# One decoder layer on a NeuronCore: the last projection block of head 0 moved ahead of the product that spreads the running maximum

## The chip, the cores and the metric

The kernel runs on one core of a Trainium2 chip, in one launch. The metric is the device time in microseconds (us): the median of three runs, beside the time and the trace of one profiled execution. The engines are called PE (TensorE, matrix products), DVE (VectorE), ACT (ScalarE), POOL (GpSimd) and SP (SyncE, which issues most DMAs). Each takes its instructions in a fixed order and waits on semaphores for the others.

## The reference, cut to what matters

One layer of a decoder, 512 positions by 1024 channels. A mixer with two groups of heads is followed by a feed-forward part with a short convolution. The group that the change touches is the mLSTM group: 4 heads of 256 channels, in chunks of 128 positions, stabilised by a running maximum.

```python
q_, k_, v_, i_, lf_ = inp
b = jnp.cumsum(lf_, axis=-1)
dmat = jnp.where(causal, b[..., :, None] - b[..., None, :] + i_[..., None, :], -jnp.inf)
m_t = jnp.maximum(b + m[..., None], jnp.max(dmat, axis=-1))
...
scores = jnp.einsum("bhtd,bhsd->bhts", q_, k_) * jnp.exp(dmat - m_t[..., None])
...
h = num / jnp.maximum(jnp.abs(den), jnp.exp(-m_t))[..., None]
...
h = rms_norm(h, ml_norm_g[l].reshape(H, Dh)).reshape(Bsz, S, D_ML)
h = (h * jax.nn.sigmoid(o_pre.astype(jnp.float32))).astype(x.dtype)
```

q, k and the output gate o_pre come from one projection of the normed input; q and k pass a causal convolution of width 4. The other group is a gated causal convolution of width 31 over 1024 channels.

## The kernel before, in words

Nearly everything is kept in 32 bits; a projection multiplies split operands, three matmuls for one product (`mm3`, L186 to L190: high by high, high by low, low by high). A weight piece of 512 columns is split by ACT into its high part (L170) and by POOL into its low part (L171).

The order of PE and of SP is the order in which the program is written. On DVE, ACT and POOL the instructions are put in order at build time, by a planner that estimates when each can run and that prefers what stands earlier in the program. What lies in a stretch of lowered priority (`tc.cur_priority += LATER`) fills gaps: above all the convolution of width 31 (L641 to L677), of whose 31 taps 25 for each block of channels are DVE instructions on L661, one after the other into a PSUM bank `cv`, while 5 run on ACT (L655) and POOL (L657) and one on ACT alone (L649); the sums ydl (L671), ysum and ysq follow. The resulting order is fixed in the program: at run time an engine never skips a waiting instruction.

Around the change, in the order of PE:

- `head_proj(0, 0)` to `head_proj(0, 2)`: a block of 24 matmuls each, for q and k of head 0. A block's result lies in one of four PSUM banks (`mm`); q and k are then convolved by ACT and DVE (`conv4`, L412 to L415), and a gate block (the fifth and sixth) only gets a tanh on ACT (L442, tile `so`).
- `fcum` (L550): the cumulated forget gates; DVE makes `ga` from them (L553). `head_proj(0, 3)`.
- `aT` (L558): `ga` is turned; DVE finds the running maximum `Mr` by a scan (L560), ACT and DVE write its high and low part into `Ms` (L562, L563). `head_proj(0, 4)`.
- `mtok` (L568): the maximum per position; from it DVE and ACT make `em` (L570 to L572).
- `make_E(0)` (L531 to L542): the product `Mb` (L533) spreads row 0 of `Ms` over 128 partitions, into one of two PSUM banks of the kind `at`; DVE adds the causal mask (`Md`, L535); ACT makes seven exponentials `E` from `Md` and `Mb` (L540, L542).
- `head_proj(0, 5)`: the last block of head 0, its second gate block.
- Then the loop over heads (L705): the blocks of head 1 alternate with the steps of `attention(0)`. The first of these are the score products `s` (L455, in `at` banks), which DVE multiplies into `E` (L456), and the products `o` (L466). ACT reads these, POOL makes the factor `fac` (L477 to L479), DVE scales the four tiles `hn` with it (L482), and PE turns them (`hT`, L488). The blocks for v of head 1 stand before and after `hT`.

Of the kernel before, what the change touches and what calls it, by code (L numbers as in the profile page):

```python
# [52 lines left out]
def decoder_layer(ctx, tc, w_glu0, x, c, adaT, vecs, w_glu, w_qko, w_v0, w_v, w_out, w_up, w_down, out):  # L53
# [30 lines left out]
    def slot(name, dt=F32):  # L84
        return slots.tile([P, T], dt, tag="t", name=name)

    def mmbank(name):
        return psum.tile([P, T], F32, tag="mm", bufs=4, name=name)

    def atbank(name):  # L90
        return psum.tile([P, T], F32, tag="at", bufs=2, name=name)
# [265 lines left out]
    def proj(ps, pieces, off):  # L357
        for k in range(KT):
            mm3(ps, blk(pieces, off + k), u[k], k == 0, k == KT - 1)
# [48 lines left out]
    def conv4(ps, i, name):  # L408

        t = slot(f"{name}c")  # L410
        w = lambda tap: vcol("qk_conv_w", tap * 16 + i)
        S.activation(t, ps, AF.Identity, bias=vcol("qk_conv_b", i), scale=w(3))  # L412
        for d in range(1, 4):
            V.scalar_tensor_tensor(out=t[:, d:], in0=ps[:, : T - d], scalar=w(3 - d), in1=t[:, d:], op0=ALU.mult, op1=ALU.add)
        S.activation(t, t, AF.Silu)  # L415
        return t
# [13 lines left out]
    def head_proj(h, i):  # L430

        pieces, qs, ks, so = heads[h]
        ps = mmbank(f"qko{h}_{i}")
        proj(ps, pieces, i * KT)
        e = 2 * h + i % 2
        if i < 2:
            qs.append(conv4(ps, e, f"q{h}_{i}"))
        elif i < 4:
            ks.append(conv4(ps, 8 + e, f"k{h}_{i}"))
        else:  # L440
            t = slot(f"so{h}_{i}")
            S.activation(t, ps, AF.Tanh, scale=0.5)  # L442
            so.append(t)
# [76 lines left out]
    def head_tiles(name, dt, three=None):  # L520
        three = three or [slots.tile([P, T], dt, tag="t", name=f"{name}{i}") for i in range(3)]
        return [three[s][:, a : a + n] for (s, a), n in zip(PLACE, NS)]
# [8 lines left out]
    def make_E(h):  # L531
        mb = atbank(f"Mb{h}")
        PE.matmul(mb, rowsel[:, h : h + 1].to_broadcast([P, P]), Ms, start=True, stop=True)  # L533
        md = slot(f"Md{h}")
        V.tensor_tensor(out=md.rearrange("p (t m) -> p t m", t=NT), in0=mb.rearrange("p (t m) -> p t m", t=NT),  # L535
                        in1=cmask[:, None, :].to_broadcast([P, NT, P]), op=ALU.add)
        E[h] = head_tiles(f"E{h}", F32)
        for cc in range(NT):
            b = ga[:, cc, h : h + 1]
            S.activation(E[h][cc][:, :P], md[:, cc * P : (cc + 1) * P], AF.Exp, bias=b, scale=-1.0)  # L540
            if cc < NT - 1:
                S.activation(E[h][cc][:, P:], mb[:, (cc + 1) * P :], AF.Exp, bias=b, scale=-1.0)  # L542
# [28 lines left out]
    S.activation(em, em, AF.Exp, scale=-1.0)  # L571
    V.tensor_scalar(out=em, in0=em, scalar1=EPS**0.5, scalar2=None, op0=ALU.mult)  # L572

    make_E(0)
    head_proj(0, 5)


    RD = float(D) ** 0.5
# [632 lines left out]
```

## Time and profile before

| | us |
|---|---|
| median of 3 runs (lowest to highest) | 786.16 (785.89 to 786.79) |
| profiled execution, its own time | 785.76 |
| its span, first to last instruction | 784.0 |
| PE busy in the span | 762.9 (97%) |
| DVE busy | 591.6 (75%) |
| ACT busy | 408.1 (52%) |
| POOL busy | 383.9 (49%) |

Times in the views are counted from the start of the span. In a timeline a row gives start, duration, engine, line, operation and tiles, with a count when like instructions follow each other, and in brackets the idle time of the engine before it and what ended that. In the view of stretches of time each engine has its busy time and the number of its instructions, and the granted clock of PE stands before the DMA's share.

### The profile page before, as it was taken

Reading aid. Unit: us, or ns where it says so; the run is one execution under the profiler, and the core shown is the slowest. Engines: PE = TensorE matmul, PEld = TensorE weight load, DVE = VectorE, ACT = ScalarE, POOL = GpSimd, SP = SyncE. Lnnn points to the kernel's source line nnn. Section 1 sums busy time; section 2 is a strip of 40 time slices with the busy share of each in tenths; the row PEclk is TensorE's granted clock in tenths of the full one; section 3 lists DMA queues with packets and bytes.
Section 4 is the critical chain, followed back from the end, with each engine's and each line's share of the span. In section 5 each row is a group of like instructions: output and inputs, shape, how many; then the busy total and the mean of one; then the engine's idle time right before and its main releaser. Section 6 shows DMA issues by size and latency. Waiting matters only on the chain.

```text
span 784.0 us, 10572 instructions
## 1 busy us (share of the span) xinstructions
PE 762.9 (97%) x3683; PEld 636.5 (81%) x3683; DVE 591.6 (75%) x938; ACT 408.1 (52%) x766; POOL 383.9 (49%) x313
## 2 busy tenths in 40 slices
PE   7899999899999999999999999999999999999995
PEld 4678888678978888888888998888888888888884
DVE  6659999999998532565868798666555687698996
ACT  6566437667765544572244445444444444456752
POOL 3689758779779544334661446444544440000001
PEclk9999999999999999999999999999999999999998
DMA  8974213302116422334953763332333321778862
GB/s 292 326 274 145 93 71 108 134 28 107 54 54 234 165 89 104 114 110 155 398 176 124 253 217 135 128 123 81 120 114 128 128 91 58 279 257 259 285 222 107
DMA packets 35977, 124.28 MB, mean 159 GB/s; under 512 B 4146, under 2 KB 5586, under 8 KB 29908
## 3 DMA queue, kind: packets, MB, share of 16 engines
q1 hardware_dynamic: 24084, 95.15, 34.7%
q10 hardware_dynamic: 11840, 28.46, 10.2%
q8 instruction: 29, 0.48, 0.2%
q14 instruction: 24, 0.20, 0.1%
HBM read 112.17 MB, written 11.42 MB: 158 GB/s over the span
## 4 chain that ended last, share of the span: by engine, by line
PE 72%; DVE 17%; DMA 4%; ACT 3%; POOL 2%; issue 1%; SPq 0%; DVEq 0%; POOLq 0%; ACTq 0%
PE up L189 10%; PE up L190 10%; PE up L188 10%; DVE cv L661 8%; PE p L190 4%; PE p L189 4%; PE p L188 4%; PE glu L189 3%; DMA wglu<-in_w_glu 2%; PE glu L190 2%; PE glu L188 2%; PE mixa L190 2%; PE mixa L188 2%; PE mixa L189 2%; PE mixb L190 2%; PE mixb L189 2%
## 5 line engine op out<-in xcount | busy, mean ns | idle before, releaser
L661 DVE SCALAR_TENSOR_TENSOR cv<-gt,cvw,cv 128x506 f32<-128x506 f32 (+24 forms) x200 | 134.1, 727 | 0.4
L617 POOL TENSOR_TENSOR ro0r<-ro0t,mhalf 128x1 f32<-128x1 f32 x1 | 0.9, 926 | 125.9 <-DVE ro0t L615 125.9
L171 POOL TENSOR_TENSOR wup_1024l<-wup,wup_1024h 128x512 fp32r<-128x512 f32 x20 | 27.3, 1367 | 31.7 <-ACT wup_1024h L170 31.7
L171 POOL TENSOR_TENSOR wup_0l<-wup,wup_0h 128x512 fp32r<-128x512 f32 x20 | 27.8, 1388 | 29.9 <-ACT wup_0h L170 29.9
L657 POOL TENSOR_TENSOR cs<-cs,cs 128x510 f32<-128x510 f32 (+3 forms) x32 | 41.9, 1308 | 0.2
L171 POOL TENSOR_TENSOR wup_1536l<-wup,wup_1536h 128x512 fp32r<-128x512 f32 x20 | 28.1, 1405 | 27.4 <-ACT wup_1536h L170 27.4
L189 PE MATMUL up<-u2l,wup_0h 128*128 128x512 f32 (+1 forms) x100 | 36.5, 365 | 0.2 <-DVE u2l L830 0.2
L188 PE MATMUL up<-u2h,wup_0h 128*128 128x512 f32 (+1 forms) x100 | 36.6, 366 | 0.0
L188 PE MATMUL up<-u2h,wup_1024h 128*128 128x512 f32 (+1 forms) x100 | 36.5, 365 | 0.0
L190 PE MATMUL up<-u2h,wup_0l 128*128 128x512 f32 (+1 forms) x100 | 36.4, 364 | 0.0
L190 PE MATMUL up<-u2h,wup_512l 128*128 128x512 f32 (+1 forms) x100 | 36.4, 364 | 0.0
L190 PE MATMUL up<-u2h,wup_1536l 128*128 128x512 f32 (+1 forms) x100 | 36.4, 364 | 0.0
L188 PE MATMUL up<-u2h,wup_1536h 128*128 128x512 f32 (+1 forms) x100 | 36.4, 364 | 0.0
L189 PE MATMUL up<-u2l,wup_1024h 128*128 128x512 f32 (+1 forms) x100 | 36.4, 364 | 0.0
L189 PE MATMUL up<-u2l,wup_1536h 128*128 128x512 f32 (+1 forms) x100 | 36.4, 364 | 0.0
L188 PE MATMUL up<-u2h,wup_512h 128*128 128x512 f32 (+1 forms) x100 | 36.4, 364 | 0.0
L189 PE MATMUL up<-u2l,wup_512h 128*128 128x512 f32 (+1 forms) x100 | 36.4, 364 | 0.0
L190 PE MATMUL up<-u2h,wup_1024l 128*128 128x512 f32 (+1 forms) x100 | 36.4, 364 | 0.0
L155 DVE SCALAR_TENSOR_TENSOR junk<-ada,cb 128x1024 bf16<-128x1024 f32 x20 | 31.3, 1565 | 6.4 <-DMA ada<-in_adaT 6.2
L171 POOL TENSOR_TENSOR wup_512l<-wup,wup_512h 128x512 fp32r<-128x512 f32 x20 | 27.2, 1361 | 14.6 <-ACT wup_512h L170 14.6
L655 ACT ACTIVATE cs<-gt,cvw 128x511 f32<-128x511 f32 (+4 forms) x40 | 27.2, 712 | 4.5 <-POOL cs L657 3.8
L171 POOL TENSOR_TENSOR wqko_1024l<-wqko,wqko_1024h 128x512 fp32r<-128x512 f32 x12 | 16.6, 1382 | 22.4 <-PE v L189 12.3
(1061 smaller groups left out, 2685.1 us busy)
## 6 DMA issues: line engine op xcount, KB each, us to landing
wup<-in_w_up SPq DMA_DIRECT2D x22, 1024.0 KB, 7.0
wqko<-in_w_qko SPq DMA_DIRECT2D x12, 1024.0 KB, 5.0
ada<-in_adaT ACTq DMA_DIRECT2D x20, 512.0 KB, 5.9
ada<-in_adaT SPq DMA_DIRECT2D x16, 512.0 KB, 5.9
wo<-in_w_out SPq DMA_DIRECT2D x8, 1024.0 KB, 9.0
spare<-in_adaT ACTq DMA_DIRECT2D x12, 512.0 KB, 7.5
wglu<-in_w_glu SPq DMA_DIRECT2D x5, 1024.0 KB, 8.4
wd<-in_w_down SPq DMA_DIRECT2D x6, 768.0 KB
```

The lines of the kernel that those rows point to most:

```text
L155: t = V.scalar_tensor_tensor(out=junk, in0=r, scalar=1.0, in1=cb, op0=ALU.mult, op1=ALU.mult, accum_out=mod[:, i : i + 1])
L171: (eng or G).tensor_tensor(out=lo[:, :n], in0=src, in1=hi[:, :n].bitcast(F32), op=ALU.subtract)
L188: PE.matmul(ps, a[0], b[0], start=start, stop=False)
L189: PE.matmul(ps, a[0], b[1], start=False, stop=False)
L190: PE.matmul(ps, a[1], b[0], start=False, stop=stop)
L617: G.tensor_tensor(out=r, in0=t, in1=mhalf[:, :1], op=ALU.pow)
L655: S.activation(t[:, d:], cvx[j][:, : T - d], AF.Copy, scale=w(CK - 1 - d))
L657: G.tensor_tensor(out=side[:, d:], in0=side[:, d:], in1=t[:, d:], op=ALU.add)
L661: last_tap = V.scalar_tensor_tensor(out=cp[:, d:], in0=cvx[j][:, : T - d], scalar=w(CK - 1 - d), in1=cp[:, d:], op0=ALU.mult, op1=ALU.add)
```

## The change

One call moves. `head_proj(0, 5)` is written ahead of `make_E(0)` instead of behind it; no instruction is added or taken away.

```diff
     S.activation(em, em, AF.Exp, scale=-1.0)
     V.tensor_scalar(out=em, in0=em, scalar1=EPS**0.5, scalar2=None, op0=ALU.mult)
 
+    head_proj(0, 5)
     make_E(0)
-    head_proj(0, 5)
```

## The prediction

> **What bounds the kernel now.** I read the page first, then who waited for whom on PE (TensorE), then the timelines of PE and DVE (VectorE) around the edited lines, and last the chain that ended last between 150 and 270 us. On the page:
>
> ```profile
> span 784.0 us, 10572 instructions
> PE 762.9 (97%) x3683; PEld 636.5 (81%) x3683; DVE 591.6 (75%) x938; ACT 408.1 (52%) x766; POOL 383.9 (49%) x313
> DVE  6659999999998532565868798666555687698996
> ```
>
> PE looks like the bound of the whole, 97%. But the DVE row, in slices of 19.6 us, stands at 9 from the fourth slice to the thirteenth: from 59 to 255 us DVE is full as well. The edit lies at 150 to 161 us, inside that stretch. Who waited for whom on PE:
>
> ```profile
> PE Mb L533 <- DVE Ms L563: 2.4, 1, 2.4
> ...
> PE hT L488 <- ACT E L542: 0.4, 1, 0.4
> PE up L189 <- DVE u2l L830: 0.2, 1, 0.2
> ```
>
> The rows left out are waits of the opening. So in the body PE has one real stop: the product of L533 that spreads the running maximum, which waits for Ms. The PE timeline shows it and what follows:
>
> ```profile
> 150.73 1.05 PE L568 MATMUL mtok<-ident,Mr 4*128 4x4 f32 x8
> 154.16 0.77 PE L533 MATMUL Mb<-Ms,rowsel 128*128 128x512 f32 x1 [2.38 <-DVE Ms L563]
> 154.73 0.63 PE L188 MATMUL qko<-uh,wqko_1024h 128*128 128x512 f32 x1
> ...
> 157.16 0.40 PE L188 MATMUL qko<-uh,wqko_1024h 128*128 128x512 f32 x1
> 157.39 0.39 PE L189 MATMUL qko<-ul,wqko_1024h 128*128 128x512 f32 x1
> ...
> 161.25 0.39 PE L188 MATMUL qko<-uh,wqko_0h 128*128 128x512 f32 x1
> ```
>
> The stop costs more than its 2.38 us. Between the start of Mb (154.16) and 157.16 stand Mb and six matmuls of the last block: 3.00 us for seven, where the usual step between two starts is 0.23 us (157.16 to 157.39), 1.6 for seven. So 1.4 us go to a slow clock, which the windows of 3.4 us show as granted (the figure of 1.00, then 0.50, before the DMA columns):
>
> ```profile
> 150.20:153.60 3.40, 1.58 (x11) 1.14 (x9) 3.37 (x5) 3.40 (x7) 2.56 (x3) 1.00 0.00 0
> 153.60:157.00 3.40, 2.83 (x7) 2.29 (x8) 3.37 (x7) 0.95 (x3) 0.23 (x1) 0.50 0.46 154
> 152.00:211.00 59.00, 56.84 (x274) 47.57 (x275) 58.94 (x94) 41.34 (x84) 46.04 (x39) 0.97 0.20 72
> ```
>
> The third row is the one that decides: from 152 to 211 us PE is busy 56.84 of 59.00, and DVE 58.94. DVE has nothing to spare there, and its order is fixed. At the end of that stretch PE needs DVE:
>
> ```profile
> 205.63 5.20 DVE L661 SCALAR_TENSOR_TENSOR cv<-gt,cvw,cv 128x501 f32<-128x501 f32 x8
> 210.75 1.12 DVE L482 TENSOR_SCALAR hn<-hn,fac 128x256 f32<-128x256 f32 x4
> 211.57 1.12 PE L488 MATMUL hT<-ident,hn 128*128 128x128 f32 x8
> ```
>
> The transposes of head 0 (hT, L488) read the four scaled tiles hn (L482), which DVE writes from 210.75 to 211.87, behind eight convolution taps (L661). PE starts them at 211.57, while DVE is still at the last tiles: at this place PE and DVE come out level. The chain that ended last says the same; between 150 and 270 us its longest pieces are DVE's taps:
>
> ```profile
> 160.60 7.66 DVE cv L661 x12
> 205.70 5.13 DVE cv L661 x8
> ```
>
> **The change, part by part.** The last block of head 0's projections (24 matmuls, head_proj(0, 5)) now stands ahead of make_E(0): Mb, the masked copy Md on DVE, seven exponentials E on ACT (ScalarE). In the order of the built program PE's only move is Mb from before these 24 to after them; SP's order does not change, so no DMA moves; on POOL (GpSimd) two neighbours change places. DVE keeps its order but for Md, which falls seven places back, behind em (L572) and six convolution taps. ACT does the last gate (so, L442) and three others ahead of the exponentials.
>
> *The stop.*
>
> ```profile
> 137.71 1.29 POOL L171 TENSOR_TENSOR wqko_1536l<-wqko,wqko_1536h 128x512 fp32r<-128x512 f32 x1
> 152.34 1.68 DVE L563 TENSOR_TENSOR Ms<-Mr,Ms 4x512 fp32r<-4x512 f32 x1
> ```
>
> When mtok ends (151.78) PE can start its 24 matmuls at once; the last piece of their weights was split by 139.00. The 18 of them that ran at full clock took 161.25 - 157.16 = 4.09, 0.227 each, so Mb is reached at 151.8 + 24 x 0.227 = 157.2. Ms is ready at 154.02 and Mb no longer waits. PE wins 2.38 + 1.4 = 3.8 us at 161.25.
>
> *The exponentials come later.*
>
> ```profile
> 157.98 0.69 DVE L535 TENSOR_TENSOR Md<-Mb,cmask 128x512 f32<-128x512 f32 x1
> 159.31 0.39 ACT L540 ACTIVATE E<-Md,ga 128x128 f32<-128x128 f32 x1
> 161.26 0.40 ACT L540 ACTIVATE E<-Md,ga 128x128 f32<-128x128 f32 x1
> 166.66 0.63 ACT L170 ACTIVATE wqko_1536h<-wqko 128x512 fp32r<-128x512 f32 x1 [2.09 <-PE qko L189]
> 168.40 0.81 PE L455 MATMUL s<-q_0c,k_2c 128*128 128x384 f32 x2
> 169.47 0.68 DVE L456 SCALAR_TENSOR_TENSOR E<-s,E 128x512 f32<-128x512 f32 x1
> ```
>
> Twelve taps take 7.66 us (the chain, above), 0.64 each. Md now comes after six of them and em: from 157.98 that is 3.8 + 0.7, so 162.5 to 163.2. The seven exponentials take 161.66 - 159.31 = 2.35 us and end near 165.5. Mb is done by 157.6, so Md holds up nothing on DVE. Behind the exponentials on ACT stand two weight pieces of head 1; the second started at 166.66 after 2.09 us of idleness, which takes the delay. Two things need the exponentials. DVE's product E (169.47) has 4 us in hand. The second score product of PE (168.40) must take over Mb's bank, since there are two banks of that kind, so it waits until ACT has read Mb for the last time, 0.3 before the end, 165.2. PE would come there at 168.40 - 3.8 = 164.6 and waits 0.6. This new wait is paid out of the 3.8: 3.2 are left.
>
> *What is late next.* With 3.2 us in hand PE runs to hT and arrives at 208.4. The hn tiles are where DVE's fixed order puts them, and DVE had no idle time to close (58.94 of 59.00, the same instructions). So PE waits there some 3 us, and of the 3.8 us nothing is left. The stop has moved from 152 to 208; in between DVE sets the pace.
>
> *The clock at the new stop.*
>
> ```profile
> 266.77 0.44 PE L488 MATMUL hT<-ident,hn 128*128 128x128 f32 x2 [0.42 <-ACT E L542]
> ```
>
> The old stop of 2.38 us halved the clock for the next 3.4 us, and that cost was covered, since PE was ahead of hn anyway. The new stop is longer, and what follows it on PE is back to back up to 266.77, where the one other wait is 0.42 us (hT <- E). Price by the rows above: 1.4 us lost after a stop, less 0.4 idle that absorbs it, so 1.0. Its ends: 0, if the clock is not halved or the work finds more cover, and half of a whole window, 1.7, less 0.4, so 1.3. I take 1.0, since the row of the old stop is the nearest and the new stop is longer. The Trainium skill ("TensorE: Matmul & The Clock Gate", HAM oscillation) asks for a PE idle gap of more than about 3.4 us before the clock falls. The trace disagrees, since 2.38 us sufficed; by the rule this stop of some 3 us would cost nothing, a rival below.
>
> *DVE's own time.* The same work can take longer or shorter by where it meets POOL:
>
> ```profile
> 158.03 1.29 POOL L657 TENSOR_TENSOR cs<-cs,cs 128x510 f32<-128x510 f32 x1
> 159.28 1.29 POOL L675 TENSOR_TENSOR ysq<-ysq,ydl 128x512 f32<-128x512 f32 x1
> 159.87 0.73 DVE L572 TENSOR_SCALAR em<-em 128x16 f32<-128x16 f32 x1
> L671 DVE SCALAR_TENSOR_TENSOR ydl<-ysum,gt x3: 683/1091/1456, 156.0 to 196.5; 128x512 f32<-128x512 f32 x3
> 196.16 1.28 POOL L171 TENSOR_TENSOR wqko_1536l<-wqko,wqko_1536h 128x512 fp32r<-128x512 f32 x1 [0.17 <-ACT wqko_1536h L170]
> 196.53 1.46 DVE L671 SCALAR_TENSOR_TENSOR ydl<-ysum,gt 128x512 f32<-128x512 f32 x1
> ```
>
> em has 16 columns and takes 0.73 us: it ends at 160.60, with the POOL instruction that runs since 159.28. The three ydl (L671) have one shape and take 0.68, 1.09 and 1.46; the last, at 196.53, ends with its compute 0.55 us after the POOL instruction that began at 196.16. So a DVE instruction whose operands all lie in SBUF waits for the POOL instruction that runs. The Trainium skill ("SBUF — State Buffer", Who interferes with whom) says so too: one port pair is locked for a whole instruction, and whoever issues first holds it; the rows agree, and by it the sum moves with the phase. Without Md ahead of it em comes 0.6 us earlier, at 159.27, within 0.02 us of the moment when POOL changes instructions (159.28): it saves 0.57 or ends where it did, with Md's 0.6 still to come. But ydl at 196.53 has 0.9 us of waiting in it, and a shift of DVE by half a microsecond either way vanishes there. I take 0; the ends are -1.2 (em, and the 0.41 that ydl of 1.09 holds, and then some, saved) and +1.0 (one more POOL turn of 1.25 lost, less some).
>
> **The sum.** Profiled execution 785.76 us (span 784.0 and 1.8 around it): PE -3.8, the bank +0.6, the wait for hn +3.2, the clock +1.0, DVE 0: +1.0, so 786.8. The median of the runs shown, 786.16, is 0.4 above the profiled one; on that footing 787.1.
>
> **The rivals.**
> 1. The stop moves, but its slow clock costs nothing (the window falls well, or the rule cited holds): 786.2. For it: the clock row is a single case. Against it: a shorter stop was enough.
> 2. DVE meets POOL better at em and at ydl, hn lands 1.2 us earlier, PE's stop shrinks to under 2 us and the clock costs some 0.3: 785.3.
> 3. Slower: DVE loses a POOL turn on its way to hn, most likely at the ydl near 180 us (1.09) by asking just after POOL has started; it decides if hn's first tile starts after 211.2. hn +1.0, PE's stop 4 us, its clock +1.0: 788.2.
> 4. The gain survives, since something lets hn come earlier by as much: 786.16 - 3.2 = 783.0. It would need idle time on DVE between 152 and 211 us, of which the window shows 0.06 us. A change that doesn't do what it says is excluded by the order: Mb does stand behind the 24 matmuls.
>
> **How the numbers follow.** My forecast (stop moved, clock paid) 50%, rival 1 13%, rival 2 12%, rival 3 19%, rival 4 6%. About 0.2%, 1.6 us, is what a measurement of this kernel can tell from no change: below 784.6 or above 787.7. Faster: rival 4 and a little of rival 2, 7%. Slower: most of rival 3 and the upper tenth of my own case, whose clock cost reaches 1.3 and DVE up to half a microsecond more, 28%. Within: 65%. The range from 785.3 (rival 2) to 788.5 (rival 3 with a full window) leaves out rival 4 and the tails. The likeliest time is 787.1.
>
> **What would show it.** Right: no wait at L533 for Ms; matmuls at 0.23 from 152 on; a wait of about 0.6 at L455 for E L542; a wait of 2.5 to 4 us at L488 for hn (L482) near 211 us; a granted clock of 0.5 in the 3.4 us around or after it; hn within 0.5 us of 210.75; no wait or a smaller one at 266. Wrong: PE without a stop at L488, or hn moved by more than 1.5 us, or the end moved by over 2 us with the stop as described.

## The result, and the profile after

| | before | after |
|---|---|---|
| median, first comparison | 786.10 us (7 runs) | 783.52 us (7 runs, 782.93 to 784.42) |
| ratio of the runs, 95% interval | | 0.9973 (0.9964 to 0.9983) |
| median, second comparison, on another occasion | 785.49 us (35 runs) | 783.53 us (11 runs) |
| ratio, 95% interval | | 0.9985 (0.9973 to 0.9996) |
| profiled execution, its span | 785.76, 784.0 us | 782.93, 781.2 us |

The kernel became faster: its median is lower by 2.6 us in the first comparison and by 2.0 in the second. The ratios, which weigh all runs, give less, 2.1 and 1.2 us, with 95% intervals of 1.3 to 2.8 and 0.3 to 2.1. The forecast was 787.1, no change to speak of. The page of the changed kernel, with the rows that were shown of before:

```profile
span 781.2 us, 10573 instructions
PE 762.0 (98%) x3683; PEld 635.5 (81%) x3683; DVE 590.7 (76%) x938; ACT 407.6 (52%) x766; POOL 384.8 (49%) x313
DVE  6659999999999433555868798666555678698986
```

On these rows almost nothing differs. Who waited for whom on PE from 100 us on:

```profile
PE hT L488 <- DVE hn L482: 1.4, 1, 1.4
PE hT L488 <- ACT E L542: 0.2, 1, 0.2
PE up L189 <- DVE u2l L830: 0.2, 1, 0.2
```

The stop at Mb is gone, a stop at hT has come, as forecast, but of 1.4 us and not of some 3. The PE timeline, and the granted clock in the windows (before the DMA's columns):

```profile
149.76 1.05 PE L568 MATMUL mtok<-ident,Mr 4*128 4x4 f32 x8
150.74 0.50 PE L188 MATMUL qko<-uh,wqko_1024h 128*128 128x512 f32 x1
...
156.34 0.40 PE L533 MATMUL Mb<-Ms,rowsel 128*128 128x512 f32 x1
...
208.62 1.46 PE L488 MATMUL hT<-ident,hn 128*128 128x128 f32 x8 [1.35 <-DVE hn L482]
```

```profile
150.20:153.60 3.40, 3.40 (x18) 2.88 (x18) 3.37 (x4) 2.56 (x5) 2.32 (x2) 1.00 0.04 10
153.60:157.00 3.40, 3.40 (x16) 2.82 (x15) 3.37 (x8) 1.75 (x3) 1.19 (x1) 1.00 0.38 145
152.00:211.00 59.00, 57.65 (x292) 48.07 (x291) 58.97 (x99) 40.31 (x85) 45.31 (x38) 1.00 0.20 72
```

PE runs at full clock throughout, and its busy time in the stretch is the whole of it less the stop. DVE is as full as before (58.97 of 59.00). Now the DVE timeline, the rows that decide; first those of after, then two of before that the prediction did not show:

```profile
147.53 1.20 DVE L560 TENSOR_TENSOR_SCAN Mr<-aT,zero 4x512 f32<-4x512 f32 x1
158.31 0.17 DVE L572 TENSOR_SCALAR em<-em 128x16 f32<-128x16 f32 x1
160.95 0.69 DVE L535 TENSOR_TENSOR Md<-Mb,cmask 128x512 f32<-128x512 f32 x1
179.13 0.69 DVE L671 SCALAR_TENSOR_TENSOR ydl<-ysum,gt 128x512 f32<-128x512 f32 x1
194.58 0.80 DVE L671 SCALAR_TENSOR_TENSOR ydl<-ysum,gt 128x512 f32<-128x512 f32 x1
208.13 1.13 DVE L482 TENSOR_SCALAR hn<-hn,fac 128x256 f32<-128x256 f32 x4
```

```profile
148.52 1.20 DVE L560 TENSOR_TENSOR_SCAN Mr<-aT,zero 4x512 f32<-4x512 f32 x1
180.66 1.09 DVE L671 SCALAR_TENSOR_TENSOR ydl<-ysum,gt 128x512 f32<-128x512 f32 x1
```

The same instructions, but three of them are shorter: em 0.17 instead of 0.73, the ydl 0.69 instead of 1.09 and 0.80 instead of 1.46. That is 0.56 + 0.40 + 0.66 = 1.62 us. From the scan Mr to hn it is 208.13 - 147.53 = 60.60 us, and was 210.75 - 148.52 = 62.23: 1.63 us, the same. In the kernel before hT began 0.82 us behind hn's start, now 0.49: 0.33 more. So hT starts 1.96 us earlier from Mr. But hT itself now takes longer: it reads the hn tiles as they come, and the matmul behind it follows after 1.22 us instead of 0.88; first before, then after:

```profile
212.45 0.36 PE L188 MATMUL v<-wv_0h,uh 128*128 128x256 f32 x1
```

```profile
209.84 0.36 PE L188 MATMUL v<-wv_0h,uh 128*128 128x256 f32 x1
```

That matmul comes 63.93 us after Mr before and 62.31 after, 1.62 us earlier, just as hn. This is what the change brings in these profiles, and both intervals hold it. The two profiled executions differ by more, 2.83 us. Of that 0.99 lies ahead of Mr, in the opening, which the change doesn't touch; over the thirteen profiles of this study Mr began between 147.27 and 149.48, and in one with PE's order of before it began at 147.53 as well. Another 0.20 lies at the next hT, whose wait for E was 0.42 us and is 0.22, and which goes up and down between 0.22 and 0.46 us in all profiles but one.

### The profile page after: what moved, and what is told of

The parts are those of the page before. It is cut to its first block, busy times and chain, and to the rows that moved or that the text cites. A ratio compares the mean times of both kernels' runs of the same rounds, so it can differ in the third digit from the quotient of the medians.

```text
span 781.2 us, 10573 instructions
## 1 busy us (share of the span) xinstructions
PE 762.0 (98%) x3683; PEld 635.5 (81%) x3683; DVE 590.7 (76%) x938; ACT 407.6 (52%) x766; POOL 384.8 (49%) x313
## 4 chain that ended last, share of the span: by engine, by line
PE 80%; DVE 14%; DMA 2%; ACT 1%; POOL 1%; issue 1%; SPq 0%; DVEq 0%; POOLq 0%; ACTq 0%
PE up L189 10%; PE up L188 10%; PE up L190 10%; DVE cv L661 6%; PE p L190 4%; PE p L188 4%; PE p L189 4%; PE glu L189 3%; PE glu L190 3%; PE glu L188 3%; PE qko L188 3%; PE qko L189 3%; PE qko L190 3%; PE mixa L190 2%; PE mixa L188 2%; PE mixa L189 2%
```

## The experiments

Theory A: from Mr to hT DVE's fixed line sets the pace, and the gain is what DVE's line got shorter; PE's removed stop makes room. Theory B: the gain is PE's removed stop itself. In the kernels with a changed order, VectorE's, ScalarE's and GpSimd's lines are written down instruction by instruction, so that only the named exchange differs; inserted source lines shift the line numbers behind them by two or three. Since the opening varies, I read hn and hT from the start of Mr (where PE waits at hT, hT itself takes some 0.3 us longer, as above, so for those kernels the column of hn is the better measure):

| run | median us | ratio to before (95%) | Mr to hn | Mr to hT | stop at hT |
|---|---|---|---|---|---|
| before | 785.5 to 786.1 | | 62.23 | 63.05 | 0 |
| after | 783.52 | 0.9973 (0.9964 to 0.9983) | 60.60 | 61.09 | 1.35 |
| after again | 783.53 | 0.9985 (0.9973 to 0.9996) | 60.63 | 61.12 | 1.39 |
| em late | 783.90 | 0.9988 (0.9974 to 1.0001) | 61.16 | 61.65 | 1.36 |
| one more tap | 784.45 | 0.9990 (0.9980 to 0.9999) | 61.82 | 62.31 | 1.39 |
| DVE half alone | 786.27 | 1.0005 (0.9992 to 1.0019) | 62.54 | 63.36 | 0 |
| PE +1.3 late | 783.68 | 0.9972 (0.9960 to 0.9984) | 60.60 | 61.09 | 0 |
| PE +1.36 early | 784.07 | 0.9993 (0.9970 to 1.0016) | 60.61 | 61.09 | 0.20 |
| PE +3.86 early | 785.37 | 0.9995 (0.9981 to 1.0009) | 62.41 | 63.22 | 0 |
| after, Ms early | 782.88 | 0.9968 (0.9954 to 0.9983) | 59.61 | 60.09 | 0.52 |
| after, three exchanges | 781.58 | 0.9949 (0.9937 to 0.9961) | 57.80 | 59.38 | 0 |
| before, Ms early | 783.20 | 0.9971 (0.9955 to 0.9987) | 60.20 | 60.69 | 1.19 |
| before, three exchanges | 781.83 | 0.9970 (0.9942 to 0.9998) | 58.36 | 59.32 | 0 |

**The changed kernel again.**

> The changed kernel once more, as the yardstick of the other runs on this chip. Theory A (from 152 to 211 us VectorE's in-order line sets the pace; the gain is VectorE's, 0.57 us at em L572 and 0.41 and 0.66 us at two ydl L671, and TensorE's removed stop only makes room for it) and theory B (the gain is TensorE's removed stop itself, 2.38 us plus 1.4 us of halved clock, less what it waits for hn) both expect 783.5 us, 2.6 below the kernel before. Theory C (a different opening, up to about 45 us, that varies from run to run, makes a third of the difference) expects the profile's VectorE times at Ms L563 to differ from the first profile by some tenths of a us while em keeps its 0.17 us; the ratio would then lie nearer 0.9977 (1.84 us).

em, the ydl, hn and the stop come out within 0.04 us of the first profile. The median is what A and B expected; the ratio is nearer what theory C expected, since three of the eleven runs took over 785 us. The profiled execution is one of them: 785.29 us, 2.4 more than the first, and 0.6 of that lies in the opening. Most of the rest lies at 400 us, where PE waits 1.25 us for `gains`; the DVE timeline of this run, then that of the first:

```profile
397.63 1.22 DVE L782 SCALAR_TENSOR_TENSOR gains<-mod,vec 128x8 f32<-128x8 f32 x1
398.76 1.33 DVE L784 COPY gains<-mod 128x8 f32<-128x8 f32 x1
```

```profile
396.24 1.21 DVE L782 SCALAR_TENSOR_TENSOR gains<-mod,vec 128x8 f32<-128x8 f32 x1
397.38 0.16 DVE L784 COPY gains<-mod 128x8 f32<-128x8 f32 x1
```

A copy of 8 columns takes 0.16 or 1.33 us; DVE also came to this place 0.8 us later, counted from hT. Theory C is right in that other places than the change scatter from run to run, the opening being one and this another.

**em one tap later.**

```diff
 DVE: cv4 tap 128x493, cv5 tap 128x500
-em (L572)
 cv4 tap 128x492
+em (L572)
```

> The changed kernel with one step of VectorE's line exchanged: em L572 stands behind the tap that followed it, so it is asked for 0.64 us later, inside GpSimd's ysq L675. No work is added. Theory A: em takes about 0.7 us instead of 0.17, hn L482 comes at least 0.55 us later, TensorE's stop at hT L488 grows from 1.35 to about 1.9 us, and the end comes 0.5 us later (784.0); up to 1.6 us later (785.1) if the two ydl fall back as well. Theory B: 783.5, as without the exchange.

```profile
158.79 0.70 DVE L572 TENSOR_SCALAR em<-em 128x16 f32<-128x16 f32 x1
...
179.52 0.68 DVE L671 SCALAR_TENSOR_TENSOR ydl<-ysum,gt 128x512 f32<-128x512 f32 x1
```

em takes 0.70, hn comes 0.55 us later from Mr, and hT by as much (61.65 against 61.11, the mean of the two runs of after). The medians differ by 0.4 us, which alone would not be told from nothing. An exchange without added work costs what em's wait costs. The stop did not grow to 1.9: its row in the waits of PE says where the time went, to the wait for E that the prediction had priced at 0.6.

```profile
PE s L455 <- ACT E L542: 0.4, 1, 0.4
```

**One more tap on DVE.**

```diff
             last_tap = V.scalar_tensor_tensor(out=cp[:, d:], ...)
+            if (j, d) == (5, 11):
+                more = V.scalar_tensor_tensor(out=cp[:, d:], in0=cvx[j][:, : T - d], scalar=zero[:, :1], in1=cp[:, d:], op0=ALU.mult, op1=ALU.add)
```

> The changed kernel with one more tap (scalar zero, 0.64 us, operand in PSUM) in VectorE's line ahead of em L572, where Md stood before: VectorE then meets GpSimd at em and ydl as in the kernel before, with TensorE's stop at L533 still gone. This is the case of the prediction. Theory A: em 0.73 us, ydl 1.09 and 1.46 us again, hn 2.3 us later than in the changed kernel, the stop at hT grows from 1.35 to about 3.6 us, a halved clock of some 3.4 us behind it: 785.8 without that, up to 787.2 with it. Theory B: 783.5, nothing of it on TensorE's line.

hn comes 1.2 us later and so does hT, and the median is 0.9 above the changed kernel; theory B had nothing. But the 2.3 us were too much:

```profile
159.26 0.56 DVE L572 TENSOR_SCALAR em<-em 128x16 f32<-128x16 f32 x1
...
180.48 0.67 DVE L674 SCALAR_TENSOR_TENSOR ydl<-ysum,gt 128x512 f32<-128x512 f32 x1
```

em waited again, ydl did not: GpSimd's line at that place moved together with DVE's. So the ydl are not short because DVE comes earlier. Nor did the stop grow (1.39), since PE was held up at L455 by 1.1 us already.

**DVE's half of the change alone.**

```diff
 DVE, in the kernel before (PE: Mb, then head_proj(0, 5)):
-Md (L535)
 cv4, cv5 taps, em (L572), four more taps
+Md (L535)
```

ScalarE's and GpSimd's lines are the changed kernel's too, but for the place of the last gate on ScalarE. Md moves by six taps, not by the eight that the expectation names.

> The kernel before (TensorE's order untouched, Mb L533 ahead of the block) with the changed kernel's order on VectorE and GpSimd: Md L535 eight taps later and behind em L572, and on ScalarE the exponentials behind two side taps and a split. The half of the change that is VectorE's alone. Theory A: em and ydl get shorter and hn comes some 1.6 us earlier, but TensorE, 0.33 us behind hn at hT already, can't use it: 785.8 to 786.1, no stop at hT, the 2.4 us stop at Mb still there. Theory D (VectorE alone sets the pace, TensorE has room): 784.3. Theory B: 786.1.

No gain, as A and B expected; D falls. Not as A expected, hn did not come earlier either:

```profile
158.29 0.17 DVE L572 TENSOR_SCALAR em<-em 128x16 f32<-128x16 f32 x1
...
167.31 0.75 DVE L414 SCALAR_TENSOR_TENSOR q_0c<-qko,vec,q_0c 128x511 f32<-128x511 f32 x1 [0.60 <-ACT q_0c L412]
...
179.93 1.15 DVE L671 SCALAR_TENSOR_TENSOR ydl<-ysum,gt 128x512 f32<-128x512 f32 x1
...
195.85 1.46 DVE L671 SCALAR_TENSOR_TENSOR ydl<-ysum,gt 128x512 f32<-128x512 f32 x1
```

em is short, and what it wins DVE loses to a wait for q of head 1, which PE delivers late. The ydl are long. With PE's stop in place, DVE's new order is worth nothing; the runs with more work on PE show why.

**More work on PE.**

```diff
 # late: in make_v, first v block of head 1, some us ahead of hT
+            for _ in range(11 * (h == 1 and tt == 0)):
+                PE.matmul(ps[:, :n], u[0][0][:, ts], wv[0][0], start=True, stop=True)
 # early: in head_proj; 6, and in another kernel 17
+        for _ in range(6 * ((h, i) == (1, 0))):
+            PE.matmul(ps, blk(pieces, 0)[0], u[0][0], start=True, stop=True)
```

> The changed kernel with 11 more matmuls of 128x256 (0.12 us each, 1.3 us) at the head of the first v product of head 1 (their sums are overwritten), some 4 us ahead of hT L488 in TensorE's line, behind everything that GpSimd's splits wait for up to ydl. Theory A (VectorE's line sets the pace to 211 us): TensorE's stop of 1.35 us at hT shrinks to 0.1 and nothing else moves; 783.5. Theory B (TensorE's line sets the pace, its removed stop is the gain): 1.3 us later, 784.8.

> The changed kernel with 6 more matmuls of 128x512 (0.227 us each, 1.36 us) at the head of head 1's first projection block (overwritten again), at 162 us, ahead of the wait of ScalarE's and GpSimd's splits of wv for a slot. Theory A with its reason for the ydl (they are short only because TensorE frees the slot early and GpSimd's wv_4l L171 is out of the way): GpSimd's wv_4l starts up to 1.4 us later, inside or behind ydl at 179 us, which grows from 0.69 to 1.1 us or more, hn comes 0.4 to 1.1 us later and the end with it (783.9 to 784.6), with the stop at hT down to about 0.5 us. Theory A without that reason: hn where it was, 783.5. Theory B: 784.8.

> The changed kernel with 17 more matmuls of 128x512 (3.86 us) where the run before had 6 (1.36 us): TensorE from 162 us on is as late as in the kernel before, with VectorE's new order kept. It asks whether the two ydl L671 at 179 and 194 us are short because TensorE is early. If so: ydl 1.1 and 1.4 us again, GpSimd's wv_4l L171 waiting on ScalarE's split and this on TensorE, hn about 1.1 us later. If not: 0.69 and 0.80 us and hn where it was. Both theories have TensorE 2.5 us late at hT (3.86 less the 1.35 of the stop), so 786.1, no stop there.

The late 1.3 us vanish in the stop: Mr to hT 61.09, as without them, and 783.68. This is where theory B falls. The early 1.36 us change nothing up to hT either, so the ydl do not hang on the last microsecond of PE's lead (that kernel's times scatter from 782.87 to 791.41 us, and its median says little). Its profiled execution lost time elsewhere, behind hT, at the transposes of head 1, where PE stood for 2.15 us; I did not follow what made E late there:

```profile
265.81 0.66 PE L490 MATMUL hT<-ident,hn 128*128 128x128 f32 x4 [2.15 <-ACT E L544]
```

With 3.86 us the ydl do change:

```profile
180.10 1.15 DVE L673 SCALAR_TENSOR_TENSOR ydl<-ysum,gt 128x512 f32<-128x512 f32 x1
...
196.02 1.45 DVE L673 SCALAR_TENSOR_TENSOR ydl<-ysum,gt 128x512 f32<-128x512 f32 x1
```

```profile
178.69 0.63 ACT L170 ACTIVATE wv_4h<-wv 128x512 fp32r<-128x512 f32 x1 [0.48 <-PE qko L189]
...
179.40 1.30 POOL L171 TENSOR_TENSOR wv_4l<-wv,wv_4h 128x512 fp32r<-128x512 f32 x1 [0.57 <-ACT wv_4h L170]
```

ydl is asked for at 180.10, while GpSimd's split of a v weight runs since 179.40, and waits it out. The split is late since ScalarE's half waited for PE. In the changed kernel nobody waits for PE there, and the split ends as ydl comes (179.13):

```profile
177.88 1.28 POOL L171 TENSOR_TENSOR wv_4l<-wv,wv_4h 128x512 fp32r<-128x512 f32 x1
```

hT starts 2.1 us later and the matmul behind it 1.8, not 2.5 (785.37 against the expected 786.1). hn is 1.8 later, more than the two ydl lost (1.1); DVE waits for q of head 1 here as well (0.41 us). So PE's removed stop does reach DVE, by way of the split weights and GpSimd. No run moved a split alone; this path is read from the timelines.

The second ydl hangs on PE in the same way, and here the kernel before shows it. These are its two ScalarE splits, then the second of them in the changed kernel, with the row that it follows:

```profile
179.20 0.63 ACT L170 ACTIVATE wv_4h<-wv 128x512 fp32r<-128x512 f32 x1 [0.43 <-PE qko L189]
195.45 0.63 ACT L170 ACTIVATE wqko_1536h<-wqko 128x512 fp32r<-128x512 f32 x1 [0.63 <-PE qko L189]
```

```profile
191.48 0.60 ACT L663 ACTIVATE gt<-cv 128x512 f32<-128x512 f32 x1 [2.58 <-DVE cv L661]
192.83 0.62 ACT L170 ACTIVATE wqko_1536h<-wqko 128x512 fp32r<-128x512 f32 x1
```

From the start of the split of `wqko_1536` on ScalarE to hn it is 15.30 to 15.33 us in every profile but the two with three exchanges. So what holds up this split sets the time of hn. In the kernel before, with DVE's half alone and with PE +3.86 it waits for PE, 0.62 or 0.63 us, and starts 46.93, 47.24 and 47.10 us after Mr; hn follows it, at 62.23, 62.54 and 62.41. In the changed kernel ScalarE waits for DVE's taps instead, and the split starts at 45.30. Theory A, that DVE's line alone sets the pace, is therefore right for the changed kernel and not for the kernel before: there DVE, busy throughout, was held at ydl by GpSimd, GpSimd by ScalarE, and ScalarE by PE. That is why DVE's half alone gained nothing, and why the change needs both halves.

**Other exchanges on DVE's line.**

```diff
 DVE: k_3c tap 128x511
+Ms (L563)
 cv4, cv5 taps, k_3c tap 128x510
-Ms (L563)
 ...                                  # and, in the kernels with three exchanges:
 ydl5
+v's ones (L395)
 memset, cv7 tap 128x505
-v's ones (L395)
 cv6 tap 128x496
+dm (L476)
 cv7 tap 128x504
-dm (L476)
```

> The changed kernel with VectorE's Ms L563 three taps earlier in its line, where GpSimd has nothing running (0.72 us idle ahead of its split at 150.0 us): 0.6 us in place of 1.7. TensorE's line is the same. Theory A: VectorE's line gains 1.0 us, hn and the exponentials with it, TensorE's stop at hT falls towards 1.35 or stays (it waits for E at L455 as well), and the end is 1.0 us earlier: 782.5. Theory B: TensorE had no wait for Ms any more, so 783.5.

> The kernel of the run with Ms early, and two more of VectorE's small steps of 0.08 us exchanged with their neighbours so that they don't wait out a GpSimd instruction: the ones of v L395 (0.82 us) right behind ydl at 195 us, where GpSimd idles, and dm L476 (1.28 us) one tap earlier. No work is added or taken away. Theory A: VectorE's line gains up to 1.0 + 0.7 + 1.2 us; TensorE has room for 1.35 of it, so the end is 1.0 to 1.6 us earlier than in the changed kernel (781.9 to 782.5) and the stop at hT is gone. Theory B: 783.5.

> The kernel before (Mb L533 ahead of the block) with VectorE's Ms L563 three taps earlier, as in the run on the changed kernel. Ms is then ready some 0.8 us before TensorE comes to Mb, so TensorE's stop of 2.38 us and its halved clock go without the change under study. Theory A: VectorE's line decides again; it gains 1.0 us at Ms, and 1.07 more if the two ydl are short wherever TensorE is early: 783.7 to 784.8 where the kernel before stands at 785.8, with a new stop at hT L488. Theory B (TensorE's removed stop is the gain): 3.8 us earlier, 782.0, no stop at hT.

> The kernel before with the three exchanges of the fastest run so far (Ms three taps earlier, the ones of v behind ydl, dm one tap earlier), TensorE's order untouched. Theory A: VectorE's line gains 2.8 us and up to 1.07 at ydl, TensorE 3.8 us, so the end is 2.8 to 3.8 us earlier than the kernel before, 782.0 to 783.0; what the change under study adds on top is em's 0.57 us, within 0.6 us of the run with the same exchanges on the changed kernel. Theory B: 782.0.

Ms alone brings 1.0 us from Mr to hT on the changed kernel, as A said, though PE had no wait for Ms left to lose (782.88). (The profile puts the 0.52 us at hT down to ScalarE's copy of v; hT starts 0.48 us behind hn there as in the other kernels that wait for hn.) All three bring 2.8 us to hn; the start of hT uses 1.7 of them and the matmul behind it 2.1, and PE then sets the pace, the stop gone:

```profile
149.63 0.68 DVE L563 TENSOR_TENSOR Ms<-Mr,Ms 4x512 fp32r<-4x512 f32 x1
...
194.49 0.16 DVE L395 COPY v<-ones 128x8 f32<-128x8 f32 x1
...
195.86 0.15 DVE L476 TENSOR_TENSOR dm<-dm,em 128x4 f32<-128x4 f32 x1
...
205.52 1.39 DVE L482 TENSOR_SCALAR hn<-hn,fac 128x256 f32<-128x256 f32 x4
```

781.58 us in six runs, 1.9 below the changed kernel and the lowest median of the study. On the kernel before, Ms early removes the stop at Mb in another way, and the ydl are short there too (0.68 and 0.79): 783.20, somewhat better than A expected and as good as the change, with a stop at hT (1.19 us) that theory B excludes. With all three it is 781.83 (780.55 to 791.95) and 59.32 to hT, against 59.38 with the change. Once DVE meets GpSimd well, the change under study adds nothing that these runs can measure.

## Why the prediction was wrong, point by point

1. *The stop at Mb and its slow clock go*: right, no wait at L533 and a clock of 1.00. Head 1's first block on PE began at 156.57 instead of 161.25, 4.68 us earlier, 0.99 of which is the opening: 3.7, said was 3.8.
2. *A new wait of 0.6 for E at L455*: too big. PE's lead shrinks there from 4.68 to 4.46, 0.2. The wait is there as soon as Md comes later (0.4 and 1.1 us with em late and with the tap).
3. *PE waits at hT, since DVE had no idle time to close*: the step that failed. The place is right and the size is not, 1.35 us against 3.2. The window row (58.94 of 59.00 busy) was read as 58.94 us of work, and "in between DVE sets the pace" rests on that. It was work and waiting: the waits for GpSimd are inside the durations, and in the kernel before the ydl waited, through GpSimd and ScalarE, for PE itself. The waits went down by 1.62 us and hn came earlier by that. hT started 0.33 us nearer to hn, but took 0.34 longer, so of the 3.7 us that PE won 1.62 was left.
4. *The clock at the new stop, +1.0*: did not come. It hung on point 3. Stops of 1.2 to 1.4 us left the clock at 1.00 in all profiles that had one behind the opening; the stop at Mb (2.38 and 2.39 us) halved it in both profiles that had it, and so did the 2.15 us at 265.81 in PE +1.36 early. The Trainium skill ("TensorE: Matmul & The Clock Gate", HAM oscillation) puts the limit at gaps of more than about 3.4 us. These three stops are shorter, so the measurement speaks against that limit here.
5. *DVE's own time, 0, with ends of -1.2 and +1.0*: the term of the sum that was mis-sized, -1.63. The mechanism stood in the text, and em's 0.57 was even worked out (measured 0.56). The error was to let it vanish at the second ydl, "a shift of DVE by half a microsecond". The ydl did not hang on DVE's shift (the tap moved DVE by 1.2 us and they stayed short) but on GpSimd's, and I moved only DVE in thought. I followed PE's lead of 3.8 us to the next wait on PE and not to the engines that wait for PE: ScalarE for a slot, GpSimd for ScalarE, ydl for GpSimd. The rows were there, with waits of 0.43 and 0.63 us of ScalarE's splits for PE.

The sum gave 786.8 for the profiled execution, and it took 782.93. Of the 3.8 us between them 1.6 is DVE's own time, 1.0 the clock that did not fall, 1.0 the opening and 0.2 the wait at the next hT. The last two scatter from run to run and are not the change's: that they fell on this side is luck. The 0.6 for the bank was too big by 0.4, without effect, since PE waits for hn behind it anyway. Rival 2 had the mechanism with too little of it (785.3), rival 4 the size (783.0) while asking for idle time that DVE did not need. Both together were given 18 in 100.

## What to carry to other kernels

Where a full engine can be held up inside its instructions by another, read its busy time as work plus waiting: a row of 16 columns that takes 0.7 us, or a group of one shape with 0.7, 1.1 and 1.5, is time that an exchange of two neighbours can free. When a stop is taken from one engine, follow its lead also to the engines that wait for it, until it comes back to the line that sets the pace. A gain can need both halves of a change, and a place that looks like its cause (the stop at Mb) can be removed in another way for the same gain.

## What the runs showed of the hardware

- A DVE instruction whose inputs all lie in SBUF waits out the GpSimd instruction that runs, whatever its size: 8 columns took 0.16 or 1.33 us, dm's 4 columns 0.15 or 1.28, Ms 0.68 or 1.7. Asked for at the end of a GpSimd instruction it is not held up, even where GpSimd's next one is ready: then that one is held up instead (GpSimd's sum `cs` behind the short ydl at 179 us took 1.87 us, where others take 1.28). This is what the Trainium skill says ("SBUF — State Buffer", Who interferes with whom): the one that issues first holds the shared pair for its whole instruction. The convolution taps, with one operand in PSUM, kept their 0.64 us next to the same GpSimd instructions, and the memset of `cs`, which has no input, its 0.06 us.
- This can make the kernel's time scatter in steps: the same program lost 1.2 us at the copy of `gains` in one execution and not in another.
- PE's granted clock fell to 0.50 for about 3.4 us after stops of 2.15, 2.38 and 2.39 us, and stayed at 1.00 after six stops of 1.19 to 1.39 us.
